# Where the small parts of the weights are subtracted: GpSimd's share of the work set to zero

## The chip, the cores and the metric

The kernel runs on one core of a Trainium2 chip. The core has a matrix engine (PE, whose loading of weights is shown apart as PEld), a vector engine (DVE), an activation engine (ACT), GpSimd (POOL) and a queue that issues transfers (SP). Each works through its own list of instructions in order. The operands lie in SBUF, the on-chip memory, and the results of products in PSUM banks. The metric is the device time of one launch in microseconds; it is the median over several runs.

## The reference

The reference takes 256 tokens of 1024 features through two blocks of two layers each, all in fp32. A layer of the first block is `x + mix(rmsnorm(x) @ w_in) @ w_out`: the projection is cut into the inputs of four small mixers, which are a convolution module of width 31 with a layernorm and a gate, a gated convolution of width 3, a windowed attention with rotary embedding, and a two-dimensional neighbourhood attention with a learned bias. A layer of the second block is a feed-forward `x + 0.5 * (silu(h @ wg) * (h @ wu)) @ wd` with 2816 hidden features, a mixing layer (an attention with forget gates, a dilated attention and a gated linear recurrence, each on its part of one projection), and a second feed-forward. A norm follows each block.

```
for l in range(DEPTH):                       # first block
    x = hybrid_layer(x, ...)
x = rmsnorm(x, final_norm_g)
for i in range(DEPTH):                       # second block
    x = x + 0.5 * _swiglu(_rmsnorm(x, ffn1_norm[i]), ...)
    x = x + _mixing(_rmsnorm(x, mix_norm[i]), ...)
    x = x + 0.5 * _swiglu(_rmsnorm(x, ffn2_norm[i]), ...)
return _rmsnorm(x, final_norm)
```

## The kernel before, in words

All products are made from operands that are split in two: a large part that the matrix engine's fast fp32 format holds exactly (`hi`), and the small rest (`lo`). A product is hi x hi plus hi x lo plus lo x hi, three passes (lines 554 to 579 and 709 to 719). The activations are split where they are made. The weights come from memory as plain fp32 and are split on the chip.

The weights are one stream of chunks of up to 128 x 2080, in the order of use. `weight_loads` (line 593) brings a chunk into one of three staging buffers `st` over SP's queue. `weight_splits` (line 610) then makes its parts, in two pieces a chunk (four in the first two chunks), so that most pieces are 128 x 1024: an ACT copy at line 620 rounds the piece into `hi`, and a subtraction at line 624, `lo = st - hi`, gives the rest. There are three `hi` and three `lo` buffers, so the splitting can run ahead of the products by up to three chunks. When the last piece is subtracted the staging buffer goes back to the loads.

The engine of the subtraction is chosen by a running share. `self.share` is set at the start of each stage, to SHARE_A in the layers of the first block (line 1267), SHARE_F in a feed-forward (line 945) and SHARE_B in a mixing layer of the second (line 1687). For every piece the share is added to `owed`; when that reaches one, one is taken off and the piece goes to GpSimd, otherwise to the vector engine. The first three chunks always go to the vector engine.

```
self.owed += self.share
self.owed, on_pool = (self.owed - 1.0, True) if self.owed >= 1.0 else (self.owed, False)
way = self.G if on_pool and i >= FAST else self.V
yield way("tensor_tensor", lo[:, s], st[:, s], hi[:, s].bitcast(F32), op=ALU.subtract)
```

These are lines 621 to 624. All vector and GpSimd instructions are recorded by one helper (line 493), all ACT instructions by another (line 470), so that the profile tells them apart by tiles.

The order of the work is written by a planner when the program is built (`Scheduler`, line 256). Each strand of work (the weight loads, the weight splits, the products, an evacuation, an attention head pair, the recurrence) is a task that offers its next instruction. The planner keeps an estimated clock for each engine and estimates from the operands when each offered instruction could start; it takes the one with the earliest such time less a priority (line 368), and appends it to its engine's list. The estimate of a vector or GpSimd instruction grows with its elements (lines 480 to 491) and knows nothing of what the two engines do to each other. A few products of two tensors (`VG`, line 503) may go to either engine, whichever comes out sooner. The engines themselves wait only for data, in the order so written.

Of the other work on the vector engine these tiles matter below. `ca` is the wide convolution of the first block (line 1106): 31 taps by two feature tiles, one instruction of 128 x 256 each, that run through the middle of the layer. `ck` holds the rotated keys of the windowed attention (line 1147), for which PE's score products wait. `sp` is the recurrence's decay in the second block, with multiplications of tile `lev` on GpSimd beside it. `sqa` collects the sums of squares for the next norm at the end of a stage (line 795), on GpSimd. `x` is the residual stream, updated from the banks of the output projection (line 750).

Of the kernel before, what the change touches and what calls it, by code (L numbers as in the profile page):

```python
# [18 lines left out]
T = 256  # L19
# [28 lines left out]
def out_order(nk, late):  # L48
    """(feature tile, k) of an output projection; the first tiles take the late k in a second sweep."""
    if not late:  # L50
        return [(fo, i) for fo in range(KT) for i in range(nk)]
    return ([(fo, i) for fo in range(OPEN) for i in range(nk - late)] +
            [(fo, i) for fo in range(OPEN) for i in range(nk - late, nk)] +
            [(fo, i) for fo in range(OPEN, KT) for i in range(nk)])
# [19 lines left out]
def weight_plan():  # L74
    """Chunks of the weight stream in the order of use: (key, source, layer, blocks);
    a block is (rows, columns) and lands as [128, len(columns)]."""
    plan = []

    def rows(k):
        return np.arange(k * P, k * P + P)  # L80

    def t_group(key, src, l, cols):
        plan.append((key, src, l, [(rows(k), cols[f:f + P]) for f in range(0, len(cols), P) for k in range(KT)]))

    def n_group(key, src, l, cols, k0=0, k1=KT):
        plan.append((key, src, l, [(rows(k), cols) for k in range(k0, k1)]))

    def o_group(key, src, l, rowlist, late):
        bl = [(rowlist[i], np.arange(fo * P, fo * P + P)) for fo, i in out_order(len(rowlist), late)]
        for c in range(0, len(bl), 16):  # L90
            plan.append((f"{key}{c // 16}", src, l, bl[c:c + 16]))

    for l in range(2):
        vcols = np.concatenate([cols_a("c_v"), cols_a("d_v")])
        n_group("v0", "w_in", l, vcols, 0, 4)
        n_group("v1", "w_in", l, vcols, 4, 8)
        for n in ORDER_A:
            t_group(n, "w_in", l, cols_a(n))
        rl = []
        for k in K_OUT_A:  # L100
            r = rows(k)
            if k in (4, 5):
                r = 4 * P + HEAD_ORDER[(k - 4) * P:(k - 3) * P]
            rl.append(r)
        o_group("o", "w_out", l, rl, LATE_A)
    for l in range(2):
        for half in (1, 2):
            for j in range(NF // 2):
                t_group(f"g{j}", f"ffn{half}_w_gate_2", l, np.arange(j * 256, j * 256 + 256))
                t_group(f"u{j}", f"ffn{half}_w_up_2", l, np.arange(j * 256, j * 256 + 256))  # L110
            o_group("d", f"ffn{half}_w_down_2", l, [rows(k) for k in range(NF)], 0)
            if half == 1:
                n_group("hi0", "w_in_2", l, cols_b("hi0"))
                n_group("hi1", "w_in_2", l, cols_b("hi1"))
                for n in ORDER_B:
                    if n in ("fv", "dv"):
                        n_group(n, "w_in_2", l, cols_b(n))
                    else:
                        t_group(n, "w_in_2", l, cols_b(n))
                o_group("o", "w_out_2", l, [rows(k) for k in K_OUT_B], LATE_B)  # L120
    return plan
# [6 lines left out]
def const_arrays():  # L128
    """Tables that depend on the shapes alone."""
# [36 lines left out]
def param_columns(g):  # L166
    """Small parameters, features on partitions (layout only)."""
# [40 lines left out]
SHARE_F = 0.25  # L208
SHARE_A = 0.6
SHARE_B = 0.45  # L210
# [45 lines left out]
class Scheduler:  # L256
    """Orders the instructions of concurrent tasks (generators) by the estimated time at which each could start.
    Only the order follows from the estimates; every wait that the data needs is Tile's."""
# [20 lines left out]
    def advance(self, t):  # L279
        """Runs a task up to its next instruction, or until it has to wait."""  # L280
# [117 lines left out]
class Builder:  # L398
# [104 lines left out]
    def VG(self, meth, out, *ins, **kw):  # L503
        """On the vector engine or, when that is done sooner, on GpSimd."""
        w, i = self._v("V", meth, out, ins, kw)
        w2, _ = self._v("G", meth, out, ins, kw)
        return Op([w, w2], [extent(out)], i)
# [28 lines left out]
    def MMs(self, products):  # L536
        """Products on distinct parts of the array, in one go: (out, lhsT, rhs, start, stop) each."""
# [16 lines left out]
    def MM3(self, out, ah, al, bh, bl, first, last):  # L554
        """Product of operands given as sums of two parts, less the product of the small parts."""
# [11 lines left out]
    def MMW(self, bank, wh, wl, x, first, last):  # L567
        """wh and wl against the parts x: [128, 2, 256], the bank's halves being the parts of the result."""
# [67 lines left out]
    def take(self, key):  # L636
        """The parts of the next chunk, its tiles, and the events of its pieces."""
# [12 lines left out]
    def dense_t(self, key, act, ready=None):  # L650
        """Features on partitions: a bank [128, nf, 256]."""
# [15 lines left out]
    def dense_w(self, key, act, ready):  # L667
        """Features on partitions: per feature tile a bank with the two parts of the result."""
# [13 lines left out]
    def dense_n(self, keys, act, width, ready=None):  # L682
        """Tokens on partitions: two banks, or halves of one, [128, width]."""
# [37 lines left out]
    def out_proj(self, key, act, nk, korder, late, coef, st, ready):  # L721
        """x += coef * act @ w, and the next norm's operands as the feature tiles finish."""
# [40 lines left out]
    def pair(self):  # L763
        """Operands of a product: large parts, small parts, and both side by side, [128, 8, 2, 256]."""
# [6 lines left out]
    def prep(self, st, fo):  # L771
        """x*g in two parts and the sums of squares, for feature tile fo."""
# [26 lines left out]
    def token_cols(self, tiles, out):  # L799
        """Sums over the partitions of [128, 256] tiles: [128 tokens, 2] in PSUM."""  # L800
# [10 lines left out]
    def bcast_cols(self, r, out):  # L811
        """[128 tokens, 2] to [128, 256] in PSUM, the same row on every partition."""
# [7 lines left out]
    def rstd(self, st, use):  # L820
        """st["r"]: [128 tokens, 2]; st["rbc"]: the same as rows, [128, 256], and what the phase asks for."""
# [131 lines left out]
    def heads(self, f, qT, kT, v, bias, nkeys, done, sink=None):  # L953
        """Heads 2f, 2f+1 (halves of feature tile f): qT(half, t), kT(half, n), v(kt, half), bias(half, t);
        done(bank) takes the bank with the outputs [128 (half, d), 256 queries]."""
# [62 lines left out]
    def rope(self, bank, ps, nf, cos, sin, o, tags):  # L1018
        """Rotary embedding of [128, nf, 256] with features on partitions, whose pairs lie 32 apart; o may hold the
        result."""  # L1020
# [14 lines left out]
    def mix_a(self, l, st, nxt):  # L1035
        nc, tc, s = self.nc, self.tc, self.s
        done = Event()
        with tc.tile_pool(name="mixa", bufs=1, reuse_waits="tile") as mp:
# [54 lines left out]
            def a_v(bank, ps):  # L1093
                """Raw like a_u: the norm's factor is applied here, to both."""
# [190 lines left out]
    def block_b_consts(self):  # L1285
        """Angles of the partial rotary embedding and the columns of the lower bounds."""
# [13 lines left out]
        # the angle over 2 pi modulo 1 with exact products: the angle in halves of 12 bits, 1 / 2 pi in three parts  # L1300
# [48 lines left out]
        # L = ln(max(lb, 1e-30)) in two steps that stay in the table's range  # L1349
# [11 lines left out]
    def mix_b(self, l, st, nxt):  # L1361
        nc, tc, s = self.nc, self.tc, self.s
        done = Event()
        with tc.tile_pool(name="mixb", bufs=1, reuse_waits="tile") as mp:
# [29 lines left out]
            def log1p_exp(ps, nch, cols=None):  # L1394
                """ln(1 + exp(-|z|)) for z and, given columns, for z + column."""
# [48 lines left out]
            def mixed(tl, m):  # L1444
                """Left halves of blocks of 2m from slot 0, right halves from slot 1."""
# [6 lines left out]
            def blocks(bank, t, left, right):  # L1452
                """left^T right within blocks of 64 tokens: [128 (block, s), (t, head), 64]."""
# [49 lines left out]
            def recurrence():  # L1503
                """A^T[s, t] of the gated recurrence: the diagonal, then pairs that meet in blocks of 2m tokens."""
# [120 lines left out]
            def dilated(f):  # L1625
                """One softmax over the keys of the three patterns, each key with its multiplicity."""
# [70 lines left out]
    def start(self, st):  # L1697
        """Loads, constants and the first norm's operands."""
# [35 lines left out]
    def warm(self):  # L1734
        """Keeps the tensor engine busy until the first operands are there, so that its clock is up by then."""
# [14 lines left out]
    def rescale(self, st, gf):  # L1750
        """x becomes the first block's output."""
# [9 lines left out]
    def last_prep(self, st, fo):  # L1761
        """x*g with tokens on partitions, and the sums of squares."""
# [74 lines left out]
def device_arrays(g):  # L1837
    """The arrays of the launch, laid out for it."""
# [3 lines left out]
    at = 0  # L1842
# [45 lines left out]
```

## Time and profile before

| | |
|---|---|
| median of 3 runs | 1400.74 us |
| lowest and highest run | 1397.69 and 1403.88 us |
| span of the profiled execution | 1401.3 us (the page gives no other time for it) |
| PE busy | 1296.3 us, 93% of the span |
| DVE busy | 1009.0 us, 72% |
| ACT busy | 776.4 us, 55% |
| GpSimd (POOL) busy | 556.5 us, 40% |

The span is the time from the first to the last instruction of one profiled execution. Busy times of different engines overlap. In time order the stages are two layers of block 1 (to 167 and to 320 us), then in each layer of block 2 a feed-forward, a mixing layer and a second feed-forward (to 523, 674 and 862, then to 1050, 1201 and 1401 us). Windows count from the span's start. [...]

### The profile page before, as it was taken

Reading aid. Unit: us, or ns where it says so; the run is one execution under the profiler, and the core shown is the slowest. Engines: PE = TensorE matmul, PEld = TensorE weight load, DVE = VectorE, ACT = ScalarE, POOL = GpSimd, SP = SyncE. Lnnn points to the kernel's source line nnn. Section 1 sums busy time; section 2 is a strip of 40 time slices with the busy share of each in tenths; the row PEclk is TensorE's granted clock in tenths of the full one; section 3 lists DMA queues with packets and bytes.
Section 4 is the critical chain, followed back from the end, with each engine's and each line's share of the span. In section 5 each row is a group of like instructions: output and inputs, shape, how many; then the busy total and the mean of one; then the engine's idle time right before and its main releaser. Section 6 shows DMA issues by size and latency. Waiting matters only on the chain.

```text
span 1401.3 us, 21738 instructions
## 1 busy us (share of the span) xinstructions
PE 1296.3 (93%) x8530; PEld 1154.8 (82%) x8530; DVE 1009.0 (72%) x1478; ACT 776.4 (55%) x1277; POOL 556.5 (40%) x321
## 2 busy tenths in 40 slices
PE   8688996798989999889999999999999889999997
PEld 7677895787878789878788888888889778788886
DVE  7996789867997656778677656777656777677742
ACT  5444555355457547567555544556447667555542
POOL 5533662445324333553433323333333652433321
PEclk9888998899999999899999999999999989999999
DMA  7532543333536554323454554554554323455550
GB/s 261 188 120 72 156 157 120 120 121 120 185 122 213 202 185 151 132 80 121 158 200 183 188 203 155 204 182 181 192 191 156 126 83 127 151 182 196 193 181 31
DMA packets 39335, 220.40 MB, mean 157 GB/s; under 512 B 10176, under 2 KB 11968, under 8 KB 13760
## 3 DMA queue, kind: packets, MB, share of 16 engines
q1 hardware_dynamic: 39232, 219.01, 43.9%
q8 instruction: 67, 1.10, 0.3%
q14 instruction: 36, 0.29, 0.1%
HBM read 217.94 MB, written 1.05 MB: 156 GB/s over the span
## 4 chain that ended last, share of the span: by engine, by line
PE 62%; DVE 24%; ACT 6%; issue 5%; POOL 2%; DMA 0%; SPq 0%; DVEq 0%; POOLq 0%; ACTq 0%
PE bank L574 27%; PE bank L575 15%; DVE ca L493 6%; DVE lo L493 4%; PE bank L561 3%; PE bank L562 3%; PE bank L563 3%; PE bank L577 3%; DVE sp L493 3%; ACT hi L470 2%; PE bank L544 2%; DVE act L493 2%; PE bank L533 2%; DVE fh L493 2%; DVE x L493 1%
## 5 line engine op out<-in xcount | busy, mean ns | idle before, releaser
L493 POOL TENSOR_TENSOR lo<-st,hi 128x1024 fp32r<-128x1024 f32 (+1 forms) x142 | 354.5, 2499 | 483.4 <-ACT hi L470 481.2
L574 PE MATMUL bank<-act,hi 128*128 128x512 f32 x1456 | 524.5, 397 | 2.4 <-DVE act L493 2.3
L470 ACT ACTIVATE hi<-st 128x1024 fp32r<-128x1024 f32 (+3 forms) x416 | 428.2, 1035 | 90.3 <-PE bank L574 48.7
L575 PE MATMUL bank<-act,lo 128*128 128x256 f32 x1664 | 437.2, 283 | 5.0 <-DVE lo L493 4.2
L493 DVE TENSOR_TENSOR lo<-st,hi 128x1024 fp32r<-128x1024 f32 (+1 forms) x274 | 358.5, 1311 | 78.7 <-ACT hi L470 75.8
L575 PEld LDWEIGHTS bank<-act,lo 128*128 128x128 f32 x1664 | 315.6, 190 | 26.0 <-DVE lo L493 6.4
L574 PEld LDWEIGHTS bank<-act,hi 128*128 128x128 f32 x1456 | 276.2, 190 | 57.4 <-DVE act L493 3.6
L574 PE MATMUL bank<-ha,hi 128*128 128x512 f32 x672 | 238.1, 396 | 3.5 <-DVE ha L493 2.8
L561 PE MATMUL bank<-act,hi 128*128 128x256 f32 x720 | 214.7, 298 | 0.0
L562 PE MATMUL bank<-act,hi 128*128 128x256 f32 x720 | 205.7, 286 | 0.6 <-DVE act L493 0.6
L563 PE MATMUL bank<-act,lo 128*128 128x256 f32 x720 | 205.5, 285 | 0.0
L575 PE MATMUL bank<-ha,lo 128*128 128x256 f32 x704 | 193.3, 282 | 0.0
L574 PEld LDWEIGHTS bank<-ha,hi 128*128 128x128 f32 x672 | 126.8, 189 | 31.2 <-DVE ha L493 3.1
L561 PEld LDWEIGHTS bank<-act,hi 128*128 128x128 f32 x720 | 140.1, 195 | 6.4 <-issue 4.2
L562 PEld LDWEIGHTS bank<-act,hi 128*128 128x128 f32 x720 | 139.6, 194 | 1.1 <-DVE act L493 0.8
L563 PEld LDWEIGHTS bank<-act,lo 128*128 128x128 f32 x720 | 139.1, 193 | 0.0
L575 PEld LDWEIGHTS bank<-ha,lo 128*128 128x128 f32 x704 | 133.1, 189 | 2.8
L493 POOL TENSOR_TENSOR fs<-fs,rbc 128x512 f32<-128x512 f32 x44 | 62.0, 1410 | 114.5 <-ACT fs L470 108.0
L493 DVE SCALAR_TENSOR_TENSOR x<-bank,x 128x256 f32<-128x256 f32 x128 | 53.1, 420 | 68.7 <-PE bank L577 67.1
L493 POOL TENSOR_TENSOR sqa<-sqa,sq 128x256 f32<-128x256 f32 x60 | 54.1, 906 | 108.8 <-ACT sq L470 106.3
L577 PE MATMUL bank<-act,hi 128*128 128x512 f32 x208 | 83.1, 400 | 1.7 <-DVE act L493 1.7
L493 DVE SCALAR_TENSOR_TENSOR ca<-hp,cw,ca 128x256 f32<-128x256 f32 x120 | 81.1, 735 | 0.0
(218 smaller groups left out, 1601.4 us busy)
## 6 DMA issues: line engine op xcount, KB each, us to landing
st<-ws SPq DMA_DIRECT2D x197, 1024.0 KB, 4.8
st<-ws SPq DMA_DIRECT2D x2, 1040.0 KB, 4.8
st<-ws SPq DMA_DIRECT2D x4, 512.0 KB, 4.3
st<-ws SPq DMA_DIRECT2D x8, 192.0 KB, 5.2
nb<-rpb SPq DMA_DIRECT2D x16, 96.0 KB, 4.8
st<-ws SPq DMA_DIRECT2D x2, 768.0 KB, 4.3
out<-st SPq DMA_DIRECT2D x4, 256.0 KB, 2.8
cst<-cst SPq DMA_DIRECT2D x1, 832.5 KB, 8.7
```

What stands on the lines that cost most here:

```text
L470: return Op([("A", dur, lambda: self.nc.scalar.activation(out, in_, func, **kw))], outs, ins, ACT_SETS.get(func))
L493: return (eng, dur, lambda: fn(out, *ins, **kw)), [extent(a) for a in aps]
L533: return Op([("P", dur, lambda: self.nc.tensor.matmul(out, lhsT, rhs, start=start, stop=stop))], [extent(out)], [extent(lhsT), extent(rhs)])
L544: mm(o, l, r, start=st, stop=sp)
L561: mm(out, ah, bh, start=first, stop=False)
L562: mm(out, ah, bl, start=False, stop=False)
L563: mm(out, al, bh, start=False, stop=last)
L574: mm(out, wh, x, start=first, stop=False)
L575: mm(out[:, 0], wl, x[:, 0], start=False, stop=False)
L577: mm(out, wh, x, start=False, stop=True)
```

## The change

The three shares are set to zero. Comments and texts of functions are taken out as well, line by line, so that all lines keep their numbers.

```diff
@@ -205,9 +205,9 @@
 PARTS = {0: 4, 1: 4}
 PRIO = dict(w1=0.8, w2=-1.8, w3=0.4, epilogue=0.5, gate=1.7, up=1.5, rstd=2.0, norm=1.3, values=0.7,
             conv=0.3, att=1.8, evac=1.1, level=0.3, prep=-0.7, rec=2.3, bias=-1.3, vg=0.2)
-SHARE_F = 0.25
-SHARE_A = 0.6
-SHARE_B = 0.45
+SHARE_F = 0.0
+SHARE_A = 0.0
+SHARE_B = 0.0
 WEIGH = dict(P=0.0118, A=0.7, V=0.35, G=0.1681, D=1.0)
```

With a share of zero `owed` stays at zero, and line 623 takes the vector engine for every piece. The planner runs anew over the whole program, since its estimates of the two engines' clocks change.

## Rows read from the trace of the kernel before

**Rows 1.** Windows by stage; columns: window, length, busy time (instructions) by engine, PEclk, DMA.
```profile
0.00:167.00 167.00, 134.27 (x921) 121.26 (x921) 137.76 (x232) 81.97 (x152) 81.29 (x65) 0.92 0.46 156
167.00:320.00 153.00, 131.67 (x911) 121.50 (x911) 125.60 (x222) 75.65 (x138) 71.58 (x41) 0.90 0.40 135
320.00:523.00 203.00, 192.51 (x1077) 165.61 (x1076) 155.22 (x223) 112.27 (x170) 74.36 (x45) 0.98 0.47 171
523.00:674.00 151.00, 139.09 (x1205) 127.77 (x1204) 112.93 (x174) 100.18 (x184) 71.22 (x33) 0.94 0.35 124
674.00:862.00 188.00, 185.66 (x1061) 162.98 (x1062) 120.91 (x156) 103.62 (x151) 61.59 (x37) 0.99 0.52 187
```
**Rows 2.** Windows of narrower stretches, the same columns (PE, PEld, DVE, ACT, POOL).
```profile
36.00:106.00 70.00, 51.45 (x389) 47.70 (x390) 67.28 (x114) 29.94 (x57) 32.54 (x16) 0.86 0.45 154
190.00:262.00 72.00, 56.77 (x436) 53.33 (x436) 67.30 (x121) 32.02 (x59) 30.64 (x14) 0.88 0.37 132
400.00:470.00 70.00, 62.91 (x345) 53.10 (x344) 58.37 (x84) 47.34 (x73) 23.78 (x12) 0.98 0.51 182
575.00:610.00 35.00, 25.37 (x316) 22.47 (x315) 30.89 (x43) 16.49 (x35) 22.57 (x8) 0.84 0.22 82
```
**Rows 3.** Waits of PE, 36 to 106 then 190 to 262 us: total, times, longest.
```profile
PE bank L544 <- DVE ck L493: 12.0, 1, 12.0
PE bank L533 <- DVE ca L493: 4.7, 1, 4.7
...
PE bank L544 <- DVE ck L493: 11.2, 1, 11.2
PE bank L533 <- DVE ca L493: 4.0, 1, 4.0
```
**Rows 4.** Timelines of DVE and POOL near 212 and 250 us: start, us, instruction.
```profile
212.71 2.21 DVE L493 SCALAR_TENSOR_TENSOR ca<-hp,cw,ca 128x256 f32<-128x256 f32 x1
...
249.93 1.22 DVE L493 TENSOR_TENSOR lo<-st,hi 128x1024 fp32r<-128x1024 f32 x1
251.06 3.25 DVE L493 SCALAR_TENSOR_TENSOR ca<-hp,cw,ca 128x256 f32<-128x256 f32 x8
...
212.25 2.39 POOL L493 TENSOR_TENSOR lo<-st,hi 128x1024 fp32r<-128x1024 f32 x1 [2.72 <-ACT hi L470]
```
**Rows 5.** Groups of instructions, whole span: count | busy us, mean ns | idle before, releaser.
```profile
L493 POOL TENSOR_TENSOR lo<-st,hi 128x1024 fp32r<-128x1024 f32 (+1 forms) x142 | 354.5, 2499 | 483.4 <-ACT hi L470 481.2
...
L470 ACT ACTIVATE hi<-st 128x1024 fp32r<-128x1024 f32 x396 | 414.5, 1052 | 81.1 <-PE bank L574 48.7 <-PE bank L562 8.8 <-PE bank L717 6.8
...
L493 DVE TENSOR_TENSOR lo<-st,hi 128x1024 fp32r<-128x1024 f32 x258 | 343.0, 1332 | 72.0 <-ACT hi L470 69.2 <-issue 2.3
```
**Rows 6.** Windows of tile lo on POOL alone: window, length, POOL busy (instructions), PEclk, DMA.
```profile
36.00:106.00 70.00, 28.12 (x11) 0.86 0.45 154
190.00:262.00 72.00, 26.63 (x11) 0.88 0.37 132
320.00:523.00 203.00, 43.30 (x17) 0.98 0.47 171
523.00:674.00 151.00, 40.87 (x16) 0.94 0.35 124
```
**Rows 7.** Windows of tile ca on DVE alone, the same columns with DVE busy.
```profile
36.00:106.00 70.00, 43.89 (x63) 0.86 0.45 154
190.00:262.00 72.00, 43.85 (x63) 0.88 0.37 132
```
**Rows 8.** Chain of work that ended last, around 670 and 1197 us: start, us, what.
```profile
669.58 0.87 POOL sqa L493
...
670.89 2.12 POOL lo L493
...
673.53 0.91 POOL sqa L493
...
1197.25 2.13 POOL lo L493
```

## Prediction, made before the changed kernel ran

> **What bounds the kernel now.** I began with the windows by stage, to see which stage has an engine that is full [rows 1]. The feed-forward stage shown fifth has PE busy 185.66 of 188 us: it is limited by the matmuls, and no relief elsewhere shortens it; the later feed-forward stages are of its kind. The two mixing layers of block 1 have PE busy 134.27 of 167 and 131.67 of 153 us, with the vector engine at 137.76 and 125.60. The first feed-forward stage stands between (192.51 of 203). The mixing layer of block 2, seen fourth (its second layer is of the same length), has some slack on both PE and DVE.
>
> An average over a stage hides its dense part, so I cut narrower stretches next [rows 2]. In 36 to 106 and in 190 to 262 us, while the wide convolution (tile ca) runs, DVE is busy 67.28 of 70 and 67.30 of 72 us, and PE only 51.45 and 56.77. There the vector engine sets the pace. The list of waits says the same from PE's side: in the first stretch PE waits 12.0 us for ck and 4.7 us for ca, both made by DVE, and in the second 11.2 and 4.0 [rows 3].
>
> The question is then what fills DVE there. One convolution step normally costs little: eight of them take 3.25 us, 0.41 us each [rows 4]. But the one at 212.71 took 2.21 us, and a GpSimd subtraction ran from 212.25 for 2.39 us [rows 4]. The step, which reads and writes SBUF as the subtraction does, stood still until GpSimd's instruction was nearly over, and ended 0.28 us after it (214.92 against 214.64). **GpSimd's help is paid for by the engine that it is to help.**
>
> **The change, part by part.** It sets the three shares to zero, so that line 622 never picks GpSimd. 142 subtractions of 2499 ns mean leave GpSimd; 142 join the 258 whole pieces that DVE has now [rows 5]. Nothing else is edited, but the planner orders every engine's instructions anew from its estimates.
>
> *Cost of the added work.* A whole piece shows a duration of 1.22 us, but the next instruction began 1.13 us after it, at 251.06 after 249.93 [rows 4]; the queue is held for 1.13. Each dense stretch has 11 GpSimd pieces [rows 6], so at most 11 x 1.13 = 12.4 us are added to DVE in each (one is half as wide, so this is slightly high). [...]
>
> *What is given back.* In each stretch tile ca holds DVE for 43.89 and 43.85 us, in 63 instructions [rows 7]. At the undisturbed 0.41 us these are 25.8, so about 18 us were spent standing still, in each. Not all of it is the subtractions' fault: they are 28.12 of 32.54 us of GpSimd's busy time in the first stretch and 26.63 of 30.64 in the second [rows 2, 6], some 87%. That gives 15.7 us as the low end of what comes back. The high end is the whole time that these subtractions run, 28.12 and 26.63, since ca is not the only victim. Net of 12.4, the gain is 3.3 to 15.7 us in the first and 3.3 to 14.2 in the second. I take 7 each, nearer the low end because the ca rows are direct and a GpSimd piece seldom blocks from its first moment: together 14 us. DVE limits both stretches and PE waits for it, so I put all 14 on the path.
>
> *Ends of the mixing layers of block 2.* In the chain of work a GpSimd subtraction of 2.12 us at 670.89 lies between two additions of the norm's sum of squares (sqa), and the next addition begins at 673.53 [rows 8]. The chain has one of the same kind at 1197.25 [rows 8]. With GpSimd free the additions follow the squares at once. Up to 2.6 us each (673.53 less 670.89); below, nothing, if the squares come late. I take 2 each, 4 together. Next late is then the token sum on PE.
>
> *The first feed-forward stage.* It has 17 pieces to move [rows 6], 19.2 us of DVE time, in a stage whose last 70 us before the down projection have DVE at 58.37 and PE at 62.91 [rows 2]. Given back as above it is about even. The ends are a gain of 7.1 (all of PE's idle time there, 70 less 62.91) and a loss of 19.2 with no give-back. I take 0, as the give-back and the addition lie close to each other wherever DVE is dense.
>
> *The mixing layers of block 2.* 16 pieces each [rows 6], 18.1 us more on a DVE with 38 us idle (151 less 112.93); PE's own work covers it. If the cover is gone, it is in the recurrence, 575 to 610 us, where DVE is at 30.89 of 35 and GpSimd's remaining multiplications still block it [rows 2]. Nothing to 18.1 of loss; a gain is possible too, as GpSimd's multiplications no longer queue behind subtractions, up to PE's 9.6 us of idle time there. I take 0.
>
> *The other feed-forward stages.* Some 16 pieces each would put 18 us on a DVE of 120.91 busy in 188 [rows 1]. Nothing shows on the path; if DVE fell behind with weights, PE would wait.
>
> *Queues.* No instruction of SP's queue moves: the weight loads wait for the staging buffer, which a shorter subtraction frees earlier. In DVE's queue each moved piece waits for the ACT copy that makes its large part, and convolution steps, evacuations and softmax steps stand behind it. That wait is now 72.0 us over 258 pieces, 0.28 us each [rows 5], mostly where DVE has time.
>
> *Sum.* The profiled span is 1401.3 us; the page gives no time around it, and it stands 0.6 above the median of 1400.74. 1401.3 - 14 - 4 = **1383 us**.
>
> **Rivals.** *Heads of the vector queue (slower).* A moved piece that reaches the head of DVE's queue before its ACT copy is done holds all the rest, and the planner's estimates place it too early. Place: the dense stretches of block 1 and the first feed-forward stage, 22 + 17 = 39 pieces. If each waited for one ACT copy, 1.05 us [rows 5], that is 41 us; less the 18 of my sum, 1401.3 + 23 = 1424. It decides once the mean wait of these pieces passes 18/39 = 0.46 us. Against it: now it is 0.28, and in the convolution ready work is always there to be placed in front. For it: DVE's queue is in order, and the pieces become more frequent.
>
> *DVE simply fuller (slower).* If blocked time were not given back, because other GpSimd work took its place, the 22 dense pieces and the 17 of the feed-forward stage would cost 39 x 1.13 = 44 us: 1445. The rows on the blocked step speak against it. [...]
>
> *No difference.* DVE gets faster in the dense stretches, but PE's fixed order and the attention and norm steps after the convolution take up the gain, or the new order loses as much elsewhere: 1399. For it: PE already works 134.27 of 167 us in the first stage, and most moved pieces lie where PE is full.
>
> *A larger gain.* PE's waits for ck and ca vanish whole, 12.0 + 4.7 + 11.2 + 4.0 = 31.9 us, and the 4 of the norm ends: 1365. [...] For it: both waits are for DVE work that was stretched. Against it: ck would still come behind convolution steps.
>
> That the change does not do what it says I leave out: with shares of zero the sum never reaches one.
>
> **How the numbers follow.** The forecast, 1370 to 1393, gets 0.46; the larger gain 0.12; no difference 0.20; the heads of the queue 0.17; the fuller DVE 0.05. A measurement of this kernel tells about 0.5% (7 us) from no change. Faster by over that are the first two, 0.58; within it 0.20; slower the last two, 0.22. The range takes the larger gain's 1365 at the bottom, a little below it for the high ends of the give-back, and above it "no difference" and the milder half of the queue rival (1401.3 + 23/2 = 1413): 1362 to 1413. The forecast's own range is 1370 to 1393.
>
> **What would show it.** Right: in the dense stretches single ca steps of over 2 us are gone, and all 63 take near 26 us; PE's waits for ck and ca shrink; each stretch is some 7 us shorter; GpSimd's busy time falls by about the 354.5 us of its subtractions [rows 5], while DVE's in the stages of block 1 doesn't rise; the feed-forward stages keep 188 us. Wrong: DVE's waits for the large parts grow over 0.46 us a piece in block 1, PE waits for small parts (lo) in the first feed-forward stage, or ca steps stay stretched behind other GpSimd work.

## The result, and the profile after

The changed kernel takes 1365.43 us (median of 4 runs, 1361.67 to 1366.19) against 1399.38 before: a ratio of 0.974, 95% interval 0.9708 to 0.9772. The profiled execution took 1365.46 us with a span of 1363.7. The direction was forecast and the range holds the time, but 18 us were forecast and 34 came: about half of the gain was forecast. Below, the busy times of the page after, and the whole pieces on DVE (of the groups by shape):

```profile
PE 1291.4 (95%) x8530; PEld 1149.0 (84%) x8530; DVE 1020.3 (75%) x1616; ACT 778.8 (57%) x1278; POOL 215.6 (16%) x183
...
L493 DVE TENSOR_TENSOR lo<-st,hi 128x1024 fp32r<-128x1024 f32 x396 | 493.0, 1251 | 96.5 <-ACT hi L470 95.9
```

DVE has 138 more instructions (142 subtractions came, and in the new order four products more went to GpSimd than came from it) and is busy only 11 us longer (1020.3 against 1009.0). A whole piece now takes 1251 ns on it instead of 1332 [rows 5]. The wait for the ACT copy is 95.9/396 = 0.24 us a piece, no more than before.

The stages after, by windows that end with the last update of the residual; columns as in [rows 1], PEclk (the granted clock) as a share of full speed:

```profile
0.00:165.60 165.60, 139.89 (x922) 124.21 (x923) 127.08 (x256) 82.08 (x151) 27.62 (x42) 0.88 0.47 160
165.60:312.60 147.00, 131.54 (x903) 118.50 (x903) 117.94 (x241) 77.94 (x142) 17.29 (x23) 0.90 0.40 137
312.60:499.90 187.30, 186.98 (x1082) 163.85 (x1081) 154.65 (x241) 112.96 (x168) 26.59 (x24) 1.00 0.52 187
499.90:647.40 147.50, 137.56 (x1210) 126.53 (x1209) 118.23 (x188) 100.17 (x184) 36.03 (x20) 0.97 0.35 128
647.40:833.90 186.50, 185.70 (x1061) 163.01 (x1062) 131.30 (x173) 103.47 (x151) 23.95 (x19) 0.99 0.52 187
```

By the same marks the eight stages before were 167.2, 152.5, 203.1, 151.5, 188.1, 187.2, 151.0 and 191.3 us. They became shorter by 1.6, 5.4, **15.8**, 4.0, 1.6, 1.9, 3.5 and 3.2. So the largest part came from the first feed-forward stage, for which I had put nothing, and block 1, for which I had put 14 us, gave 7. (The two profiled executions differ by 37.6 us, the medians by 34: the one profiled before is among the longer of its kernel, so differences of a few us by stages are uncertain.)

In block 1 the mechanism is there. The steps of a convolution are no longer stretched to over 2 us (the longest takes 0.96), and its 62 take 26.3 us where [rows 7] had 43.9 (windows of tile ca on DVE):

```profile
36.00:118.00 82.00, 26.31 (x62) 0.92 0.51 176
184.00:263.00 79.00, 26.39 (x62) 0.97 0.46 168
```

Yet the convolution as a whole got longer. From its first step to the end of its last it took 64.3 and 61.0 us before, and takes 75.0 and 74.4 after. The planner now puts 22 pieces of weights between its steps, where DVE had 6 and GpSimd 9 before. PE waits less for ck and more for ca than in [rows 3] (waits of PE, 36 to 118 us, then 184 to 263):

```profile
PE bank L533 <- DVE ca L493: 8.5, 1, 8.5
PE bank L544 <- DVE ck L493: 4.2, 1, 4.2
...
PE bank L533 <- DVE ca L493: 4.6, 1, 4.6
...
PE bank L544 <- DVE ck L493: 0.9, 1, 0.9
```

The change thus did two things at once: it moved 142 subtractions to another engine, and it had the planner write another order. The experiments take these apart. The theory was that the blocked vector engine had cost the time; the rival, that the new order brought it.

### The profile page after: what moved, and what is told of

The parts are those of the page before. It is cut to its first block, busy times and chain, and to the rows that moved or that the text cites. A ratio compares the mean times of both kernels' runs of the same rounds, so it can differ in the third digit from the quotient of the medians.

```text
span 1363.7 us, 21594 instructions
## 1 busy us (share of the span) xinstructions
PE 1291.4 (95%) x8530; PEld 1149.0 (84%) x8530; DVE 1020.3 (75%) x1616; ACT 778.8 (57%) x1278; POOL 215.6 (16%) x183
## 4 chain that ended last, share of the span: by engine, by line
PE 81%; DVE 11%; ACT 3%; issue 2%; DMA 1%; SPq 1%; POOL 0%; POOLq 0%; DVEq 0%; ACTq 0%
PE bank L574 33%; PE bank L575 19%; PE bank L561 5%; PE bank L563 5%; PE bank L562 5%; PE bank L577 4%; PE bank L544 3%; DVE sp L493 2%; DVE lo L493 2%; PE bank L533 2%; PE bank L551 1%; DVE act L493 1%; PE bank L715 1%; PE bank L716 1%; PE bank L717 1%
## 5 line engine op out<-in xcount | busy, mean ns | idle before, releaser
L493 DVE TENSOR_TENSOR lo<-st,hi 128x1024 fp32r<-128x1024 f32 (+3 forms) x416 | 511.4, 1236 | 105.6 <-ACT hi L470 104.9
L561 PE MATMUL bank<-act,hi 128*128 128x256 f32 x720 | 211.0, 293 | 0.0
L562 PE MATMUL bank<-act,hi 128*128 128x256 f32 x720 | 204.8, 284 | 0.5 <-DVE act L493 0.5
L493 POOL TENSOR_TENSOR fs<-fs,rbc 128x512 f32<-128x512 f32 x44 | 65.5, 1490 | 408.0 <-ACT fs L470 408.0
L470 ACT ACTIVATE act<-x,par 128x256 fp32r<-128x256 f32 x56 | 28.1, 506 | 84.0 <-DVE x L493 81.1
L470 ACT ACTIVATE fh<-bank 128x256 f32<-128x256 f32 x88 | 33.4, 380 | 64.0 <-PE bank L577 64.0
```

The lines of the kernel that those rows point to most:

```text
L470: return Op([("A", dur, lambda: self.nc.scalar.activation(out, in_, func, **kw))], outs, ins, ACT_SETS.get(func))
L493: return (eng, dur, lambda: fn(out, *ins, **kw)), [extent(a) for a in aps]
L561: mm(out, ah, bh, start=first, stop=False)
L562: mm(out, ah, bl, start=False, stop=False)
```

## Experiments

**One engine, two orders.** In the first pair the planner plans a subtraction for one engine and the program issues it on the other. PE, ACT and SP keep exactly the order of before (first kernel) or of after (second).

```diff
-                way = self.G if on_pool and i >= FAST else self.V
-                yield way("tensor_tensor", lo[:, s], st[:, s], hi[:, s].bitcast(F32), op=ALU.subtract)
+                moved = on_pool and i >= FAST
+                yield self.subtract(moved, lo[:, s], st[:, s], hi[:, s].bitcast(F32))
+def subtract(self, moved, out, a, b):
...
+    plan, real = (wg, wv) if moved else (wv, wv)      # new_order_pool: (wv, wg)
+    return Op([(plan[0], plan[1], real[2])], [extent(out)], ins)
```

Expected of the old order with all subtractions on DVE: 

> The order of every engine's other work is that of before, and only the 142 subtractions of GpSimd run on the vector engine, at the place in the order where the planner had them. Theory of the blocked engine (the time comes from vector instructions that no longer stand still): nearly the whole gain is there, 1365 to 1375 us. Rival of the order (the time comes from the planner having ordered the work anew): little of it, 1388 to 1400 us; and if the vector engine's queue is held up by pieces that wait for their ACT copy, over 1400.

Expected of the new order with GpSimd's share: 

> The order of every engine's work is that of the changed kernel, but 142 subtractions run on GpSimd by the shares of before. Theory of the blocked engine: the gain is lost, 1395 to 1415 us, and single convolution steps of over 2 us are back. Rival of the order: most of the gain stays, 1365 to 1380 us.

Measured, in us (ratios to before 0.9545, interval 0.9506 to 0.9584, and 1.0234, interval 1.0202 to 1.0267; the 1365.43 stood beside a before of 1399.38):

| | 142 pieces on GpSimd | on the vector engine |
|---|---|---|
| order of before | 1402.28 (before) | 1336.22 |
| order of after | 1433.60 | 1365.43 (after) |

Both theories had a part, and neither had the sizes: 1336 lies below the range of the blocked engine, and 1434 above it. In either order the engine is worth 66 to 68 us. In either column the new order costs 29 to 31 us. The change gained 66 and gave 30 back. In the new order on GpSimd the stretched steps are back (duration of a ca step: least, median, most; then first and last start):

```profile
L493 DVE SCALAR_TENSOR_TENSOR ca<-hp,cw,ca x120: 471/476/2629, 47.6 to 280.4; 128x256 f32<-128x256 f32 x120
```

The stages of the old order on DVE, columns as above:

```profile
0.00:146.30 146.30, 129.76 (x921) 117.79 (x921) 128.16 (x255) 82.05 (x152) 27.67 (x43) 0.98 0.53 180
146.30:276.50 130.20, 123.13 (x910) 114.10 (x911) 117.12 (x243) 75.28 (x138) 15.38 (x17) 0.99 0.45 156
276.50:465.90 189.40, 186.65 (x1075) 162.84 (x1074) 155.08 (x240) 112.88 (x171) 30.64 (x29) 1.00 0.51 185
465.90:613.70 147.80, 136.66 (x1208) 126.36 (x1206) 116.45 (x190) 100.44 (x184) 31.84 (x18) 0.97 0.37 128
```

The two layers of block 1 are 21 and 22 us shorter than before, the first feed-forward 14. The order is the same, so DVE's instructions can be matched one by one: other than the subtractions, those from the first convolution's start to its end took 64.6 us before and take 45.0 (sums of durations), those behind it in the layer 42.2 and 32.1, and those of the first feed-forward stage 100.4 and 82.1. So the GpSimd subtractions held up much of DVE's work, not the convolution alone. Against the changed kernel the whole loss lies in block 1 (146.3 and 130.2 instead of 165.6 and 147.0).

**One kind of stage at a time.** SHARE_F alone, then SHARE_A alone, set to zero.

> The share is zero in the feed-forward stages alone. From the stages of the two traces: the four feed-forward stages are 15.8, 1.6, 1.9 and 3.2 us shorter, so about 22 us, 1377 us, if each stage gains by itself. If the first feed-forward stage gained because of the layers ahead of it, its part (15.8) stays out: about 1393 us.

> The share is zero in the two layers of block 1 alone. From the stages of the two traces: 1.6 and 5.4 us shorter, so about 7 us, 1392 us, if each stage gains by itself. By the sum of the prediction 14 us, 1385 us. If the first feed-forward stage gains from the layers ahead of it, some 16 us more: about 1377 us.

1392.26 us (ratio 0.9935, 0.9915 to 0.9955) and 1387.74 us (0.9908, 0.9884 to 0.9932): both faster, by less than 2%. The first feed-forward stage is 190.5 us in the one and 195.8 in the other, against 203.1 before and 187.3 with both: part of its gain is its own, and part comes from the layers ahead. The 1393 us expected for the case that only_ffn leaves this gain out thus came by other stages: its first mixing layer of block 2, planned anew, is 7.6 us longer. Its two layers of block 1, in which the order is that of before to the last instruction, came out 3.8 and 2.4 us shorter, so a stage's difference of that size is not to be read as an effect.

**What blocks the vector engine.** To old_order_dve, GpSimd instructions were added that compute nothing that is used: beside each moved piece three subtractions of 128 x 256 that read the large part, or one tiny subtraction and eight fills that read nothing.

```diff
...
+    def both():
+        wv[2]()
+        for _ in range(3):
+            self.nc.gpsimd.tensor_tensor(spare, b[:, :256], b[:, :256], op=ALU.subtract)
...
```

and, for idle_writes:

```diff
...
+        self.nc.gpsimd.tensor_tensor(spare[:, :8], b[:, :8], b[:, :8], op=ALU.subtract)
+        for _ in range(8):
+            self.nc.gpsimd.memset(spare, 0.0)
...
```

> As old_order_dve (1336 us), and beside each of the 142 moved subtractions GpSimd runs three subtractions of 128 x 256 that read the same large part and write a spare tile that nothing uses (some 2.2 us together). Added work alone: what the kernel computes is the same. If a GpSimd instruction that reads SBUF holds the vector engine up, the blocked time returns on top of the work that now stands there: 1390 us or more, single convolution steps of over 0.7 us, and tile ca of each convolution back over 40 us. If the time before was lost to something else (the latency of GpSimd's results), 1336 to 1345 us.

> As idle_reads, but beside each moved subtraction GpSimd runs one tiny subtraction (128 x 8) and eight fills of the spare tile, which read nothing and only write (some 2.4 us together). If it is the reading that holds the vector engine up, 1336 to 1348 us. If any GpSimd instruction on SBUF does, the same as idle_reads.

1393.38 us (ratio 0.9959, 0.9946 to 0.9972) and 1355.39 us (0.968, 0.966 to 0.97). Work of GpSimd that serves nothing costs 57 us if it reads, 19 if it almost only writes. The groups of GpSimd's added instructions, and of the ca steps, of idle_reads:

```profile
L1902 POOL TENSOR_TENSOR spare<-hi 128x256 f32<-128x256 f32 x426 | 412.1, 967 | 454.8 <-ACT hi L470 431.6
...
L493 DVE SCALAR_TENSOR_TENSOR ca<-hp,cw,ca 128x256 f32<-128x256 f32 x120 | 67.1, 612 | 0.0
```

the same of idle_writes:

```profile
L1903 POOL MEMSET spare<- 128x256 f32 x1136 | 355.8, 313 | 65.4
L1901 POOL TENSOR_TENSOR spare<-hi 128x8 f32<-128x8 f32 x142 | 108.6, 765 | 374.2 <-ACT hi L470 372.4
...
L493 DVE SCALAR_TENSOR_TENSOR ca<-hp,cw,ca 128x256 f32<-128x256 f32 x120 | 52.0, 487 | 0.0
```

and of old_order_dve:

```profile
L493 DVE SCALAR_TENSOR_TENSOR ca<-hp,cw,ca 128x256 f32<-128x256 f32 x120 | 51.1, 481 | 0.0
```

With the fills GpSimd is busy longer (356 + 109 us against 412, or 3.27 us against 2.90 for each moved piece), and the convolution steps stay at 487 ns; with the reads they go to 612 (35 us for a convolution's steps instead of 26; over 40 were expected). So what held DVE up in these runs was the GpSimd instructions of 128 x 256 that read SBUF (967 ns each), not the fills (313 ns), which only write it. (The two runs also differ in the operation, a subtraction and a fill, and no run parts the two.) The time of idle_writes, 1355, passed the range that I gave it (up to 1348). Its 19 us seem to have another place: GpSimd's needed results come later when its own queue is full, and ACT's next `hi` waits for the added instructions, as the waits of that run show (who, for whom: total, times, longest):

```profile
DVE fh L493 <- POOL fs L493: 11.9, 20, 0.6
...
PE bank L533 <- POOL sqa L493: 11.5, 3, 3.8
...
ACT hi L470 <- POOL spare L1903: 8.7, 5, 2.6
...
DVE dg L493 <- POOL sc L493: 7.4, 9, 2.2
```

In old_order_dve the second of these is 5.3 us, the last 5.2, and the other two don't appear. A second price of GpSimd's help, then, that my sum did not have: it delays the other work of GpSimd itself. How much of the 19 us each wait makes was not tested, and the third is made by the experiment itself. idle_reads has waits of the same kinds (8.3 us for sqa, 8.3 for fs, 6.8 for `hi`), so not all of its 57 us is the reading.

**Why the new order costs 30 us.** The first guess was the convolution's priority in the planner (0.3, below the 0.8 of a split that is at most one chunk ahead).

```diff
-            conv=0.3, ...
+            conv=3.0, ...
```

> The changed kernel with one number altered: the convolution's priority in the planner is 3.0 instead of 0.3, so that its steps stand ahead of other vector work that could start at the same time. Theory: the new order costs some 29 us because the subtractions and the rest are put ahead of the convolution, which now lasts 75 us; then the convolution falls to 45 to 55 us and both layers of block 1 get some 15 us shorter: 1330 to 1350 us. Rival: the new order loses elsewhere, and the convolution's earlier end only makes PE wait for weights or attention instead: 1358 to 1380 us.

1363.58 us (0.9746, 0.9724 to 0.9768): the guess falls. The convolution shrank to 24.5 us, below the range, and PE waited 22.8 and 13.5 us for it in one piece: no split stands between its steps now, and in the first layer 486 of the projection's 600 products come behind that wait. Pacing it, one step for every 0.8 or 0.9 us of the planner's vector clock, was the next:

```diff
-            prio = dict(a_u=PRIO["conv"])
+            prio = dict(a_u=self.pace)
...
+def pace(self):
+    late = getattr(self, "taps", 0) and self.s.clock["V"] - self.since > self.taps * STEP
+    return 3.0 if late else PRIO["conv"]
```

> The changed kernel, all subtractions planned and run on the vector engine; the convolution's priority is 3.0 whenever fewer steps are placed than one for every 0.8 us of the planner's vector clock since the convolution began, and 0.3 otherwise. So it neither falls behind the subtractions (75 us long in the changed kernel) nor keeps them out (24.5 us in conv_first). Theory: the new order costs what it does because the convolution ends after PE has done all products that don't depend on it; paced, the convolution lasts some 50 us, the granted clock stays up after it, and both layers of block 1 come near those of old_order_dve (146 and 130 us): 1332 to 1348 us. Rival: the loss lies in the rest of the order; 1355 to 1370 us.

> As paced_08 with one step for every 0.9 us: a convolution of some 56 us, as in old_order_dve. Theory: within 6 us of paced_08, 1332 to 1350 us. Rival: 1355 to 1370 us.

1354.14 us (0.9665, 0.9629 to 0.9701) and 1353.94 us (0.9673, 0.9657 to 0.9689): 11 of 30 us come back, between the two forecasts. The convolutions last 60.7 and 55.6 us in paced_08 and 66.1 and 61.8 in paced_09, longer than meant, but the length alone is not the matter: in conv_first it is 24.5, and nothing came back. What PE still has to do when the convolution is over is another difference. Below, windows of line 561 on PE (one of three passes of each product of the projection) up to the layernorm's product and from there to the end of the first layer: length, PE busy (instructions), granted clock, DMA. First before, then after, then old_order_dve, then paced_08:

```profile
0.00:103.20 103.20, 42.94 (x149) 0.92 0.57 193
103.20:167.20 64.00, 16.84 (x51) 0.91 0.29 97
```

```profile
0.00:116.20 116.20, 57.47 (x200) 0.93 0.60 203
116.20:165.60 49.40, 0.00 (x0) 0.74 0.18 59
```

```profile
0.00:93.20 93.20, 43.23 (x149) 0.96 0.62 204
93.20:146.30 53.10, 15.26 (x51) 1.00 0.38 138
```

```profile
103.60:161.10 57.50, 9.66 (x33) 0.91 0.39 134
```

In the old order a quarter of the products stands behind the layernorm, beside the chain of layernorm, gates and attention. In the new one none does: PE has only small products of that chain, which wait for other engines' results (1.96 us for tile th of ACT, 1.86 and 2.22 for dg and pt of DVE), and the granted clock of that window falls to 0.74, with 0.57 in its first 26 us: 0.51 up to 131.8 us, 0.94 up to 135.2, 0.50 up to 142.0 (all engines, after; then the 26 us behind the same product in old_order_dve):

```profile
116.20:142.00 25.80, 17.95 (x65) 10.77 (x66) 12.37 (x44) 11.21 (x31) 5.52 (x6) 0.57 0.00 1
```

```profile
93.20:119.20 26.00, 23.87 (x187) 21.54 (x188) 22.45 (x53) 15.66 (x35) 6.80 (x8) 1.00 0.31 117
```

PE had 65 instructions there in the one, 187 in the other. The planner takes what could start first. When it counts the subtractions on DVE, it expects vector results later and, so the theory, spends the independent products before. The last pair changes nothing against the changed kernel but that count (the edit is shown against old_order_dve).

```diff
-    plan, real = (wg, wv) if moved else (wv, wv)
-    return Op([(plan[0], plan[1], real[2])], [extent(out)], ins)
+    return Op([("V", 0.0 if moved else wv[1], wv[2])], [extent(out)], ins)   # uncounted_04: 0.4
```

> All subtractions run on the vector engine and are planned there, but for the 142 that were GpSimd's the planner counts 0 us of the vector engine's time instead of 1.13. In its order 147 of the 600 products of the first projection part still stand behind the convolution's layernorm product on PE, as in the order of before (153); in the changed kernel none does. Theory: the new order loses because the planner, counting the subtractions, puts every product that needs no vector result ahead of the layernorm, so that PE has nothing to run beside the chain that follows; then both layers of block 1 come back to some 148 and 132 us: 1333 to 1347 us. Rival (the rest of the order loses it): 1353 to 1368 us.

> As uncounted, with 0.4 us counted for each of the 142. Of the 600 products 57 still stand behind the layernorm product. Theory: between the two, nearer the changed kernel in the first layer: 1343 to 1358 us. Rival: 1358 to 1370 us.

1344.29 us (0.9594, 0.9574 to 0.9615) and 1351.10 us (0.9639, 0.9613 to 0.9664), both in the theory's range. With 1.13, 0.4 and 0 us counted, and 0, 57 and 147 of the first layer's 600 products left behind, the time goes 1365, 1351, 1344. Of the 29 us between the changed kernel and old_order_dve, 21 thus come back when the planner doesn't count the moved subtractions; the first layer is at 146.2 us, as in the old order. Of the other 8 us some 6 lie in the second layer (136.6 instead of 130.3), by stages, and were not traced further. That it is the products left behind which decide is not shown: a new count changes the whole order, and paced_08 leaves 33 of 200 on line 561, 99 of 600, and yet its first layer takes 161.1 us, while uncounted_04 with 57 takes 153.5, and paced_09 with none 159.4. Why the order written with the full count is slower stays open beyond that. The opposite excess fails as well: the planner told that all splits run on GpSimd.

> As old_order_dve, but the planner believes that all subtractions after the first three chunks run on GpSimd (shares of one), while all run on the vector engine. If the planner's order is the better the less it counts them on the vector engine: 1320 to 1336 us. If its clock of the vector engine must not be too far off, other work is placed as if the engine were free and PE waits for small parts: 1340 to 1370 us.

1373.41 us (0.9818, 0.9793 to 0.9842), above both forecasts. Against old_order_dve the first feed-forward stage takes 200.3 us instead of 189.4, and the two layers of block 1 are 13 and 7 us longer; why was not traced.

**A faster version.** In the recurrence 16 multiplications of tile lev remain on GpSimd. They were issued on DVE too, planned as before.

```diff
-                yield self.VG("tensor_tensor", ev, ev, mixed(kq, m), op=ALU.mult)
+                yield self.product(ev, ev, mixed(kq, m))
+def product(self, out, a, b):
...
+    op.ways = [(v, dv, fv), (g, dg, fv)]
...
```

> As old_order_dve (1336 us), and the 16 multiplications of tile lev in the recurrences, 2.6 us each on GpSimd, run on the vector engine at their place too, with the order of all other work kept. If what blocks the vector engine there is worth more than the work itself (its steps on tile sp average 1.56 us instead of 0.69), each of the two mixing layers of block 2 gains 2 to 6 us: 1324 to 1333 us. If a multiplication in the vector engine's own queue costs the recurrence as much as it frees: 1333 to 1342 us.

1324.56 us, ratio 0.9469 (0.9448 to 0.9491): the fastest of the study. Steps of tile sp in old_order_dve, and then both groups of levels_dve:

```profile
L493 DVE TENSOR_TENSOR sp<-sp 128x512 f32<-128x512 f32 x28 | 43.8, 1564 | 3.2 <-ACT lev L470 2.6
```

```profile
L493 DVE TENSOR_TENSOR lev<-lev,kq 128x1024 f32<-128x1024 f32 x16 | 20.0, 1252 | 0.0
L493 DVE TENSOR_TENSOR sp<-sp 128x512 f32<-128x512 f32 x28 | 19.3, 689 | 0.6 <-ACT lev L470 0.2
```

The vector engine took over 20.0 us of work and got 24.5 us back from its own 28 steps; each layer is 5 to 6 us shorter.

## Why the prediction was right in direction and wrong in size

Two terms failed. The sum put the relief of DVE at 18 us in all, and in the same order it is worth 66; and it put the planner's new order at nothing, and that took some 30 back. The forecast was nearer than its terms, since the two errors have opposite signs.

*What bounds block 1, and the blocking:* right. The convolution step that took 2.21 us was no accident; moving the readers off GpSimd gave 66 us in the same order, and reads that nobody needs, with their other costs, took 57 away again.

*The added work:* right. The next instruction that does not wait follows a whole piece after 1.13 us (the median after), as the rows said, and DVE's busy time in block 1 fell (127.08 and 117.94 us against 137.76 and 125.60).

*"All 14 on the path" in block 1:* wrong in both of its parts. Without a new order the gain was not 14 but 43 us (20.9 and 22.2 by the stages). The convolution itself gave 9.6 and 8.7 of it (54.7 and 52.3 us long instead of 64.3 and 61.0), near my 7 each. The rest lay outside the convolution, 10.9 us behind it in the first layer, 5.1 ahead of it and 8.4 behind it in the second. I had not priced that since DVE is not full there, though its instructions were held up there too (42.2 us instead of 32.1 behind the first convolution). Then the new order took 36 us of it back, and I had named that only as a sentence under "no difference".

*The first feed-forward stage at 0:* of the stages the one that failed most, with 15.8 us. I had set given-back against added DVE time, found them even, and bounded the gain by PE's idle time in 70 us (7.1). DVE's busy time did stay even (155.22 and 154.65). But equal sums say nothing of the path. PE was idle for 10.5 us in the whole stage before, waiting for late results, mostly of DVE, and for 0.3 after; the other 5.6 are PE's own busy time (192.6 before, 186.98 after), with the granted clock up from 0.98 to 1.00. The longest of PE's waits in that stage before, and the only one after:

```profile
PE bank L575 <- DVE lo L493: 4.2, 5, 1.9
PE bank L574 <- DVE ha L493: 2.8, 1, 2.8
...
PE bank L533 <- POOL sqa L493: 0.2, 1, 0.2
```

That late results came early because a blocked instruction stands still wherever GpSimd happens to be, while a subtraction goes where the planner has room, is argued; that the stage gains without a new order (13.7 us) is measured.

*The ends of the mixing layers of block 2:* right, 4 were put down and 4.2 came. PE's longest waits for the additions, 3.1 us, stand at these two ends before, and are 1.0 there after (over the whole span, before and then after):

```profile
PE bank L533 <- POOL sqa L493: 7.8, 3, 3.1
...
PE bank L533 <- POOL sqa L493: 2.2, 3, 1.0
```

In the old order without GpSimd's subtractions they are 2.3, so part of this term is the order's. The stages' own 4.0 and 3.5 us by the marks are not these waits alone, as the wait ends behind the mark.

*The other feed-forward stages at 0:* 6.7 us came in three stages, at the edge of what the stages of unchanged order vary by.

*The rivals:* the heads of DVE's queue did not stall (0.24 us a piece, against 0.46 for that to decide; the most in a stretch that the rival named is 6.0 us over 25 pieces, in the first convolution). DVE "simply fuller" fell with DVE's busy time, 11 us more for 142 pieces. "A larger gain" had the right time, 1365, by a mechanism that did not happen: of the 31.9 us of waits for ck and ca 18.2 are still there. That it hit was luck.

*The base of the sum:* a span was taken as if it were a time. Every execution of this record takes 1.7 to 2.2 us more than its span (1365.46 and 1363.7 for the one profiled after), so the execution profiled before took some 1403, 4 above the median of 1399.38. It matters little beside the two terms above.

## What to carry to other kernels

Time that one engine loses because another holds it up can't be set against work of the same length: it falls on whatever is next, so equal sums of busy time may hide a gain (here 15.8 us in one stage). When a change goes through a scheduler, test the move and the new order apart, by planning on one engine and issuing on the other. And look at what an order leaves for its serial chains: here the order that had spent all independent products ahead of the chain had PE waiting in it, at a granted clock of 0.57, though the number of products left does not by itself tell the length of the layer.

## What was not expected of the hardware

GpSimd's fills of 128 x 256 took 313 ns each, 356 us in all, and left DVE's convolution steps alone (487 ns beside 481), while a subtraction of only 128 x 8 took 765 ns. And a stretch with PE busy for 17.95 of 25.80 us, on small products alone, was granted 0.57 of the full clock, where the old order's, at 23.87 of 26.00, was granted 1.00.
